# adaLN's first shift and scale: four of eight row sums as one-column products on PE

## The chip, the cores and the metric

One core of one Trainium2 chip runs the kernel. Its engines are PE (TensorE, matrix products), DVE (VectorE), ACT (ScalarE), POOL (GpSimd) and SP (SyncE, which here only issues transfers); each works through its own queue in order. The metric is device microseconds (us) of one execution; less is better.

## The reference, cut to what matters

The kernel computes one layer of a decoder trunk for 1024 tokens of 1024 channels in float32. Only its beginning matters here:

```python
cond = jax.nn.silu(c)
mod = cond @ w_ada[layer] + b_ada[layer]
shift1, scale1, gate1, shift2, scale2, gate2 = jnp.split(mod[:, None, :], 6, axis=-1)
h = rms_norm(x, w_norm1[layer]) * (1.0 + scale1) + shift1
proj = h @ w_in        # inside hybrid_mixer
```

`c` is one vector of 1024, `w_ada` is 1024 x 6144. `shift1` and `scale1` are sums over the 1024 rows of the first 2048 columns of `w_ada`. Every channel of `h` needs its shift and scale, and every later product needs `h`.

## The kernel before

Channels lie on 128 partitions in 8 blocks k, tokens in 8 tiles t. The first stage (lines 181 to 324) loads the x tiles, normalizes them in place (`x_rows`), transposes them on PE (`x_columns`) into `hT`, and then makes `h` in two parts whose sum has float32 accuracy: `hH` (rounded to the type fp32r in which PE multiplies) and `hL` (the rest). With them it computes `wva`, 272 columns of `w_in` (the attention's values and the gates), for all tokens, as `tok_hi` (`hH` by the weights' high and low parts) and `tok_lo` (`hL` by the high part), into eight PSUM tiles `os`.

The stage runs over four groups g of two channel blocks each (`GS`). For each group:
- SP loads the group's part of `w_ada` (`ada_load`) in two pieces `wt` of 512 rows, 2 x 512 KB each; `stw` has two buffers, so a load waits until the sums over an older piece are done.
- DVE multiplies each of 8 blocks of 128 rows by the column of `cond` and adds it up in `acc`, 128 partitions x 512 columns (`ada_sums`, lines 209 and 211): eight instructions.
- PE transposes `acc` in four pieces (line 289), and DVE reduces them over the partitions that were (line 290): this gives shift and scale with channels on partitions. Two small DVE instructions (292, 294) add `b_ada` and the gain to give `sc`.
- ACT makes `hH` = `hT` x scale + shift for two blocks, then `hT` the same way in place; POOL subtracts the two to give `hL` (line 304; in the last group DVE takes the second block).
- PE runs `tok_lo` of the group before, then `tok_hi` of this one.

The split of a raw weight tile `wraw` into `wh` (ACT) and `wl` (`split`, line 61) stands in the same queues. For `wva` itself POOL does the subtraction; for the weights of the next products DVE does. The order inside this stage is the order in which the code is written; work from behind it (loads and splits of the next weights, line 134 and 61) is placed among it by a scheduler. The PSUM pools are `ps` (2 banks) and `pq` (6).

Of the kernel before, what the change touches and what calls it, by code (L numbers as in the profile page):

```python
# [9 lines left out]
F32 = mybir.dt.float32  # L10
# [4 lines left out]
OP = mybir.AluOpType  # L15
# [21 lines left out]
def hybrid_block_kernel(ctx, tc, x, c, w_in, w_out, w_mix_norm, attn_f_bias, sg_w, sg_b,  # L37
# [143 lines left out]
    with tc.tile_pool(name="st", bufs=1, side="left") as st, tc.tile_pool(name="stx", bufs=6, side="left") as stx, \  # L181
            tc.tile_pool(name="stw", bufs=2, side="left") as stw, tc.manual_schedule():
        hT = st.tile([P, KT, S], F32, name="hT")
# [9 lines left out]
        def ada_load(g, q):  # L193

            k0, k1 = GS[g]
            was[g, q] = stw.tile([P, 4, 2, (k1 - k0) * P], F32, name=f"wt{k1 - k0}", tag="wt")
            for i in range(2):
                nc.sync.dma_start(was[g, q][:, :, i], w_ada[q * 4 * P:(q + 1) * 4 * P, i * D + k0 * P:i * D + k1 * P]
                                  .rearrange("(k p) f -> p k f", p=P))

        def ada_sums(g, q):
            if q == 0:
                n = GS[g][1] - GS[g][0]
                accs[g] = st.tile([P, 2, n * P], F32, name=f"acc{n}", tag="acc", bufs=2)
            acc = accs[g]
            for k in range(q * 4, q * 4 + 4):
                wt = was[g, q][:, k % 4]
                if k == 0:
                    nc.vector.tensor_scalar(acc, wt, cond[:, k:k + 1], None, op0=OP.mult)
                else:  # L210
                    nc.vector.scalar_tensor_tensor(acc, wt, cond[:, k:k + 1], acc, op0=OP.mult, op1=OP.add)

# [23 lines left out]
        for lo, hi, src in ((8, 16, w_norm1.rearrange("o (a p) -> (o a) p", p=P)),  # L236
# [4 lines left out]
            nc.sync.dma_start(rows[lo - 8:hi - 8], src)  # L241
        ada_load(0, 0)
        for t in range(4, 7):
            x_load(t)
        ada_load(0, 1)
        x_load(7)
        wraw = [stx.tile([P, 4, 272], F32, name="wraw1", tag="xt") for _ in range(2)]
        for i in range(2):
            o = 0
            for c0, n in ((AV, 260), (MDT, 4), (LI, 8)):  # L250
                nc.sync.dma_start(wraw[i][:, :, o:o + n], w_in[i * 512:(i + 1) * 512, c0:c0 + n]
                                  .rearrange("(k p) g -> p k g", p=P))
                o += n
        wva = [wp.tile([P, KT, 272], F32R, name=f"w{s}") for s in "hl"] + [272]
        crows = st.tile([8, P], F32, name="crows")
        nc.scalar.dma_start(crows, c.rearrange("o (a p) -> (o a) p", p=P))
# [7 lines left out]
        for t in range(NT + 1):  # L264
            if t < NT:
                x_rows(t)
            if t:
                x_columns(t - 1)
            if t in (5, 7):
                ada_sums(0, t // 7)  # L270
        psc = pq1()
# [4 lines left out]
        sc = st.tile([P, 2, KT], F32, name="sc")  # L276
        os = [ps1() for _ in range(PSB)] + [pq1() for _ in range(7 - PSB)]
        NGK = len(GS)
        for g, (k0, k1) in enumerate(GS):
            ks, n = slice(k0, k1), k1 - k0  # L280
            for q in range(2):
                if g:
                    ada_sums(g, q)
                if g + 1 < NGK:
                    ada_load(g + 1, q)
            acc = accs[g]
            o = pq1()
            for i in range(2 * n):
                nc.tensor.transpose(o[:, i * P:(i + 1) * P], acc[:, i // n, i % n * P:(i % n + 1) * P], ident)
            nc.vector.tensor_reduce(sc[:, :, ks], o[:, :2 * n * P].rearrange("p (i k f) -> p i k f", i=2, k=n),  # L290
                                    axis=AX.X, op=OP.add)
            nc.vector.tensor_add(sc[:, :, ks], sc[:, :, ks],
                                 cols[:, 54:70].rearrange("p (i k) -> p i k", i=2)[:, :, ks])
            nc.vector.scalar_tensor_tensor(sc[:, 1, ks], sc[:, 1, ks], 1.0, cols[:, 8 + k0:8 + k1],
                                           op0=OP.add, op1=OP.mult)

            for k in range(*GS[g - 1]) if g else ():
                for t in range(NT - 1):
                    tok_lo(os[t], wva, t, k)
            for k in range(k0, k1):  # L300
                act(hH[:, k, :], hT[:, k, :], AF.Identity, scale=sc[:, 1, k:k + 1], bias=sc[:, 0, k:k + 1])
            for k in range(k0, k1):
                act(hT[:, k, :], hT[:, k, :], AF.Identity, scale=sc[:, 1, k:k + 1], bias=sc[:, 0, k:k + 1])
                (nc.gpsimd if g + 1 < NGK or k % 2 == 0 else nc.vector).tensor_sub(hL[:, k, :], hT[:, k, :], hH[:, k, :].bitcast(F32))

            for k in range(k0, k1):
                for t in range(NT - 1):
                    tok_hi(os[t], wva, t, k)
        os.append(pq1())
        for k in range(KT):  # L310
# [1908 lines left out]
```

## Time and profile before

| | us |
|---|---|
| median of 3 runs | 1276.43 |
| the runs | 1275.05 to 1279.74 |
| the profiled execution, own time | 1279.96 |
| its span, first to last instruction | 1278.3 |
| PE busy in the span | 1159.6 (91%) |
| DVE busy | 806.7 (63%) |
| ACT busy | 589.4 (46%) |
| POOL busy | 345.8 (27%) |

The span is what the profiler saw between the first and the last instruction; the run's own time has some 1.7 us around it. Busy shares are means over the whole kernel, so a stage with another limit is read by itself: its waits, and the timeline of each engine. `PEclk` is the share of TensorE's full clock of 2.4 GHz that was granted; it has two levels, 0.50 (1.2 GHz) and 1.00, and a value between is a mean over both.

### The profile page before, as it was taken

The numbers are of one execution on the slowest core, as the hardware profiler recorded it, in microseconds if no ns is written. First come the engines' busy times: TensorE is split into PE (matmuls) and PEld (weight loads), VectorE is DVE, ScalarE is ACT, GpSimd is POOL, SyncE is SP. The second block draws the span as 40 slices with busy tenths as digits, with TensorE's granted clock in tenths as the row PEclk, the third lists the DMA queues.
The fourth block names the chain that finished last, engine by engine and source line by source line (L and its number), as shares of the span: only waits on it lengthen the run. The fifth ranks groups of instructions, "written<-read, shape, count | busy, mean of one in ns | idle before, by whom it ended". The sixth has DMA issues, their size and how long they took to land. (4 is left out here: it accounts for less than half of the span.)

```text
span 1278.3 us, 18648 instructions
## 1 busy us (share of the span) xinstructions
PE 1159.6 (91%) x6455; PEld 872.4 (68%) x6455; DVE 806.7 (63%) x1484; ACT 589.4 (46%) x909; POOL 345.8 (27%) x331
## 2 busy tenths in 40 slices
PE   4589889999999899999959999899999999999981
PEld 3577776889998788887747744468666666666561
DVE  6976766857743488488878941335445576665675
ACT  6442114354743488444437841224324555555453
POOL 2420000002201278333321953313222322222111
PEclk8889989999999999999969999999999999999996
DMA  9614874231221123575477999999879999999985
GB/s 266 210 34 153 260 261 118 75 95 50 67 68 34 42 59 106 197 280 198 152 298 288 335 334 368 373 391 367 314 241 352 376 383 392 387 390 378 356 309 223
DMA packets 97397, 306.04 MB, mean 239 GB/s; under 512 B 15923, under 2 KB 54573, under 8 KB 72717
## 3 DMA queue, kind: packets, MB, share of 16 engines
q1 hardware_dynamic: 85050, 284.47, 60.8%
q0 software_dynamic: 9120, 17.69, 5.8%
q10 hardware_dynamic: 3122, 2.56, 0.6%
q8 instruction: 57, 0.93, 0.3%
q14 instruction: 48, 0.39, 0.1%
HBM read 283.86 MB, written 32.62 MB: 248 GB/s over the span
## 5 line engine op out<-in xcount | busy, mean ns | idle before, releaser
L1647 POOL DMA_INDIRECT x_d<-yt,tabi x34 | 62.4, 1835 | 228.8 <-DVE yt L1621 174.7
L56 PE MATMUL ps<-wu,xTs 128*64 128x512 f32 x256 | 119.5, 599 | 3.0 <-DMA wu<-in_w_expert_up_dram 3.0
L56 PE MATMUL ps<-wg,xTs 128*64 128x512 f32 x256 | 120.0, 599 | 0.0
L56 PE MATMUL ps<-wh,hH 128*128 128x256 f32 (+1 forms) x336 | 97.8, 292 | 12.3 <-ACT hH L53 5.9
L56 PE MATMUL ps<-wl,hH 128*128 128x256 f32 (+1 forms) x336 | 96.6, 288 | 0.0
L56 PE MATMUL ps<-wh,hL 128*128 128x256 f32 (+1 forms) x336 | 96.2, 291 | 0.0
L56 PE MATMUL ps<-hH,wh 128*128 128x512 f32 x224 | 89.6, 400 | 0.4 <-ACT xbc L53 0.4
L56 PE MATMUL ps<-hL,wh 128*128 128x512 f32 x224 | 89.4, 399 | 0.0
L56 PE MATMUL ps<-hH,wl 128*128 128x512 f32 x224 | 89.1, 398 | 0.0
L56 PEld LDWEIGHTS ps<-wh,hH 128*128 128x128 f32 x336 | 65.7, 195 | 15.3 <-ACT hH L53 6.5
L56 PE MATMUL ps<-split,xTH 128*128 128x512 f32 x200 | 69.4, 403 | 1.2
L1638 POOL TENSOR_TENSOR yt<-yt,g2bc 128x1024 f32<-128x1024 f32 x14 | 33.7, 2409 | 130.6 <-ACT yt L53 114.5
L56 PEld LDWEIGHTS ps<-wg,xTs 128*64 128x64 f32 x256 | 32.0, 136 | 54.2 <-issue 50.5
L53 ACT ACT_TABLE_LOAD x47 | 60.3, 1283 | 17.6 <-DVE xbc L685 5.9
L56 PEld LDWEIGHTS ps<-wl,hH 128*128 128x128 f32 x336 | 65.2, 194 | 1.7 <-issue 1.6
L53 ACT ACTIVATE xTH<-pq 128x512 fp32r<-128x512 f32 x33 | 18.4, 593 | 102.2 <-PE pq L1662 102.2
L56 PEld LDWEIGHTS ps<-wh,hL 128*128 128x128 f32 x336 | 65.4, 197 | 0.0
L56 PE MATMUL ps<-wh,xTH 128*128 128x512 f32 (+1 forms) x156 | 64.2, 412 | 1.2 <-PEq L1867 0.5
L56 PE MATMUL ps<-wl,xTH 128*128 128x512 f32 (+1 forms) x156 | 61.5, 394 | 0.6 <-DVE wl L61 0.5
L53 ACT ACTIVATE sg<-ps 128x512 f32<-128x512 f32 (+1 forms) x32 | 18.9, 592 | 92.3 <-PE ps L56 50.6
L56 PE MATMUL pq<-wd,aTs 128*64 128x512 f32 x256 | 59.0, 597 | 2.6 <-PEq L1855 2.2
L56 PE MATMUL ps<-wh,xTL 128*128 128x512 f32 (+1 forms) x156 | 60.9, 391 | 0.0
(566 smaller groups left out, 3257.2 us busy)
## 6 DMA issues: line engine op xcount, KB each, us to landing
wg<-in_w_expert_gate_dram SPq DMA_DIRECT2D x64, 1024.0 KB
wu<-in_w_expert_up_dram SPq DMA_DIRECT2D x64, 1024.0 KB
wd<-in_w_expert_down_dram SPq DMA_DIRECT2D x64, 1024.0 KB
mw<-in_w_ada_dram SPq DMA_DIRECT2D x32, 512.0 KB
wraw<-in_w_in_dram SPq DMA_DIRECT2D x20, 512.0 KB
xt<-in_x_dram SPq DMA_DIRECT2D x16, 512.0 KB
wt<-in_w_ada_dram SPq DMA_DIRECT2D x16, 512.0 KB
woraw<-in_w_out_dram SPq DMA_DIRECT2D x16, 256.0 KB
```

Of the source, the lines that this page charges most:

```text
L53: return nc.scalar.activation(o, i, f, **kw)
L56: return nc.tensor.matmul(o, l, r, start=start, stop=stop)
L1638: nc.gpsimd.tensor_mul(yt[:, on_dve * 512:], yt[:, on_dve * 512:], g2bc[:, on_dve * 512:])
L1647: nc.gpsimd.indirect_dma_start(out=x1_d, out_offset=bass.IndirectOffsetOnAxis(ap=tok, axis=0), in_=yt, in_offset=None, bounds_check=S - 1, ...
```

## The change

Half of the rows of each group, blocks k = 4 to 7, are no longer summed on DVE. `ada_columns` multiplies them on PE: the 128x128 piece of `wt` is the stationary operand and one column of `cond` the moving one, so that the result comes out as a column of `ada` with channels on partitions. The blocks k = 0 to 3 are still summed on DVE into `acc`; a fifth product with a column of ones adds this sum over the partitions. The transposes and the reduction are gone. `ada` takes one `ps` bank until the last group; `os` has one tile in `ps` and six in `pq` instead, and its eighth tile takes the bank of `ada`.

Loads come in pieces of half the rows, 2 x 256 KB, with four buffers. The load of `wva`'s raw weights is issued by POOL instead of SP. `hT` is computed by DVE instead of ACT, and `hL` is shared: POOL takes the even block, DVE the odd one. The sums of the next group stand behind this on DVE, and its columns on PE stand between `tok_hi` of this group and `tok_lo`.

The diff, cut to its core:

```diff
-            tc.tile_pool(name="stw", bufs=2, side="left") as stw, tc.manual_schedule():
+            tc.tile_pool(name="stw", bufs=4, side="left") as stw, tc.manual_schedule():
...
-            was[g, q] = stw.tile([P, 4, 2, (k1 - k0) * P], F32, name=f"wt{k1 - k0}", tag="wt")
+            was[g, q] = stw.tile([P, 2, 2, (k1 - k0) * P], F32, name="wt")
             for i in range(2):
-                nc.sync.dma_start(was[g, q][:, :, i], w_ada[q * 4 * P:(q + 1) * 4 * P, i * D + k0 * P:i * D + k1 * P]
+                nc.sync.dma_start(was[g, q][:, :, i], w_ada[q * 2 * P:(q + 1) * 2 * P, i * D + k0 * P:i * D + k1 * P]
                                   .rearrange("(k p) f -> p k f", p=P))
 
-        def ada_sums(g, q):
-            if q == 0:
...
-            for k in range(q * 4, q * 4 + 4):
-                wt = was[g, q][:, k % 4]
+        def ada_sums(g):
+
+            accs[g] = st.tile([P, 2, (GS[g][1] - GS[g][0]) * P], F32, name="acc", bufs=2)
+            for k in range(4):
+                wt = was[g, k // 2][:, k % 2]
                 if k == 0:
...
+        def ada_columns(g):
+
+            k0, k1 = GS[g]
+            n = k1 - k0
+            for i in range(2):
+                for j in range(n):
+                    o, cs = ada[:, 4 * g + i * n + j:4 * g + i * n + j + 1], slice(j * P, (j + 1) * P)
+                    for k in range(4, KT):
+                        mm(o, was[g, k // 2][:, k % 2, i, cs], cond[:, k:k + 1], k == 4, False)
+                    mm(o, accs[g][:, i, cs], ones[:, 0:1], False, True)
...
         ada_load(0, 0)
+        ada_load(0, 1)
         for t in range(4, 7):
             x_load(t)
-        ada_load(0, 1)
+        ada_load(0, 2)
         x_load(7)
+        ada_load(0, 3)
...
-                nc.sync.dma_start(wraw[i][:, :, o:o + n], w_in[i * 512:(i + 1) * 512, c0:c0 + n]
+                nc.gpsimd.dma_start(wraw[i][:, :, o:o + n], w_in[i * 512:(i + 1) * 512, c0:c0 + n]
...
+        ada_load(1, 0)
+        ada_load(1, 1)
...
-            if t in (5, 7):
-                ada_sums(0, t // 7)
+            if t == 5:
+                ada_sums(0)
+            if t == 7:
+                ada_columns(0)
...
-            for q in range(2):
-                if g:
-                    ada_sums(g, q)
-                if g + 1 < NGK:
-                    ada_load(g + 1, q)
-            acc = accs[g]
-            o = pq1()
-            for i in range(2 * n):
-                nc.tensor.transpose(o[:, i * P:(i + 1) * P], acc[:, i // n, i % n * P:(i % n + 1) * P], ident)
-            nc.vector.tensor_reduce(sc[:, :, ks], o[:, :2 * n * P].rearrange("p (i k f) -> p i k f", i=2, k=n),
-                                    axis=AX.X, op=OP.add)
-            nc.vector.tensor_add(sc[:, :, ks], sc[:, :, ks],
+            if g + 1 < NGK:
+                ada_load(g + 1, 2)
+                ada_load(g + 1, 3)
+            if g + 2 < NGK:
+                ada_load(g + 2, 0)
+                ada_load(g + 2, 1)
+            nc.vector.tensor_add(sc[:, :, ks], ada[:, 4 * g:4 * g + 2 * n].rearrange("p (i k) -> p i k", i=2),
...
             for k in range(k0, k1):
-                act(hT[:, k, :], hT[:, k, :], AF.Identity, scale=sc[:, 1, k:k + 1], bias=sc[:, 0, k:k + 1])
-                (nc.gpsimd if g + 1 < NGK or k % 2 == 0 else nc.vector).tensor_sub(hL[:, k, :], hT[:, k, :], hH[:, k, :].bitcast(F32))
+                nc.vector.tensor_scalar(hT[:, k, :], hT[:, k, :], sc[:, 1, k:k + 1], sc[:, 0, k:k + 1],
+                                        op0=OP.mult, op1=OP.add)
+            for k in range(k0, k1):
+                (nc.vector if k % 2 else nc.gpsimd).tensor_sub(hL[:, k, :], hT[:, k, :], hH[:, k, :].bitcast(F32))
+            if g + 1 < NGK:
+                ada_sums(g + 1)
...
+            if g + 1 < NGK:
+                ada_columns(g + 1)
```

In the order rows below, a name is the tile that an instruction writes, the names behind the arrow are what it reads, and a number behind a name tells tiles apart. The first place is DVE's queue for the second group, from `sc` of the first group to `sc` of the second (`wl` is the split of the next weights). Before:

```order
L294 SCALAR_TENSOR_TENSOR sc<-sc,cols 128x2
L209 TENSOR_SCALAR acc_406<-wt_358,cond 128x512
L211 SCALAR_TENSOR_TENSOR acc_406<-wt_358,cond,acc_406 128x512 x3
L211 SCALAR_TENSOR_TENSOR acc_406<-wt_361,cond,acc_406 128x512 x4
L61 TENSOR_TENSOR wl<-wraw,wh 128x4x256
L290 TENSOR_REDUCE sc<-pq_421 128x2x2
```

On the same place of DVE's queue in the changed kernel:

```order
L305 SCALAR_TENSOR_TENSOR sc<-sc,cols 128x2
L314 TENSOR_SCALAR hT<-hT,sc 128x1024 x2
L317 TENSOR_TENSOR hL<-hT,hH 128x1024
L207 TENSOR_SCALAR acc<-wt,cond 128x512
L61 TENSOR_TENSOR wl<-wraw,wh 128x4x256
L209 SCALAR_TENSOR_TENSOR acc<-wt,cond,acc 128x512 x3
L303 TENSOR_TENSOR sc<-ps_201,cols 128x2x2
```

Four sums went; `hT` twice, one `hL` and the `wl` split now stand ahead of the remaining sums.

The second place is PE's queue at the border between the first and the second group (`ps_201` is `ada`, `ps_351` and `ps_380` are the first tile of `os`). Before:

```order
L56 MATMUL pq_357<-wh,hH 128x272
L56 MATMUL pq_357<-wl,hH 128x272
L289 MATMUL pq_421<-ident,acc_406 128x128 x4
L56 MATMUL ps_351<-wh,hL 128x272
L56 MATMUL ps_352<-wh,hL 128x272
```

PE at the same border in the changed kernel:

```order
L56 MATMUL pq_386<-wh,hH 128x272
L56 MATMUL pq_386<-wl,hH 128x272
L56 MATMUL ps_201<-cond,wt 128x1 x4
L56 MATMUL ps_201<-ones,acc 128x1
L56 MATMUL ps_201<-cond,wt 128x1 x4
L56 MATMUL ps_201<-ones,acc 128x1
L56 MATMUL ps_201<-cond,wt 128x1 x4
L56 MATMUL ps_201<-ones,acc 128x1
L56 MATMUL ps_201<-cond,wt 128x1 x4
L56 MATMUL ps_201<-ones,acc 128x1
L56 MATMUL ps_380<-wh,hL 128x272
```

Four transposes became twenty one-column products, of which the fifth is the first that reads `acc`.

The third place is PE's queue at the last x tiles, ahead of the first group (`pq_315` to `pq_337`, and `pq_328` to `pq_366`, take the last two tiles' transposes). Before:

```order
L225 MATMUL pq_315<-ident,xt 128x128 x4
L225 MATMUL pq_321<-ident,xt 128x128 x4
L225 MATMUL pq_331<-ident,xt 128x128 x4
L225 MATMUL pq_337<-ident,xt 128x128 x4
L272 MATMUL pq_343<-ident,rows 128x66
L289 MATMUL pq_364<-ident,acc_288 128x128 x4
```

PE at the last x tiles in the changed kernel:

```order
L234 MATMUL pq_334<-ident,xt 128x128 x4
L56 MATMUL ps_201<-cond,wt 128x1 x4
L56 MATMUL ps_201<-ones,acc 128x1
L56 MATMUL ps_201<-cond,wt 128x1 x4
L56 MATMUL ps_201<-ones,acc 128x1
L56 MATMUL ps_201<-cond,wt 128x1 x4
L56 MATMUL ps_201<-ones,acc 128x1
L56 MATMUL ps_201<-cond,wt 128x1 x4
L56 MATMUL ps_201<-ones,acc 128x1
L234 MATMUL pq_360<-ident,xt 128x128 x4
L234 MATMUL pq_366<-ident,xt 128x128 x4
L288 MATMUL pq_372<-ident,rows 128x66
```

The first group's products moved ahead of the last x tile's transposes; in the kernel before its transposes of `acc` stood behind them.

## Rows read from the trace of the kernel before

**Rows 1.** Stretch: length, PE, PEld, DVE, ACT, POOL busy us, PEclk, DMA, GB/s.

```profile
80.00:90.00 10.00, 10.00 (x58) 8.82 (x58) 7.75 (x31) 5.52 (x13) 0.00 (x0) 1.00 0.18 49
```

**Rows 2.** Waits of 0 to 180 us: engine, line, releaser, us, times, longest.

```profile
ACT hH L53 <- DVE sc L294: 26.0, 4, 8.0
...
DVE acc L211 <- DMA wt<-in_w_ada_dram: 1.0, 2, 0.5
```

**Rows 3.** ACT's timeline: start us, us, engine, line, operation, operands, count [idle before].

```profile
36.13 2.38 ACT L53 ACTIVATE hH<-hT,sc 128x1024 fp32r<-128x1024 f32 x2 [4.65 <-DVE sc L294]
...
60.80 2.38 ACT L53 ACTIVATE hH<-hT,sc 128x1024 fp32r<-128x1024 f32 x2 [6.99 <-DVE sc L294]
...
73.44 2.37 ACT L53 ACTIVATE hH<-hT,sc 128x1024 fp32r<-128x1024 f32 x2 [7.99 <-DVE sc L294]
```

**Rows 4.** PE's timeline, 42 to 85 us.

```profile
58.56 1.09 PE L289 MATMUL pq<-ident,acc 128*128 128x128 f32 x4 [5.40 <-DVE acc L211]
...
75.25 0.36 PE L56 MATMUL ps<-wh,hH 128*128 128x272 f32 x1
```

**Rows 5.** DVE's and POOL's timeline in the third group.

```profile
51.35 7.06 DVE L211 SCALAR_TENSOR_TENSOR acc<-wt,cond,acc 128x512 f32<-128x512 f32 x4 [0.52 <-DMA wt<-in_w_ada_dram]
...
51.67 5.40 POOL L304 TENSOR_TENSOR hL<-hT,hH 128x1024 fp32r<-128x1024 f32 x2 [6.30 <-ACT hT L53]
```

**Rows 6.** Groups of instructions (busy us, mean ns), then ns min/median/max of the sums.

```profile
L218 DVE TENSOR_SCALAR xt<-xt,rstd 128x1024 f32<-128x1024 f32 x8 | 6.0, 754 | 0.3
L304 POOL TENSOR_TENSOR hL<-hT,hH 128x1024 fp32r<-128x1024 f32 x7 | 18.8, 2698 | 22.5 <-ACT hT L53 22.5
L61 DVE TENSOR_TENSOR wl<-wraw,wh 128x1024 fp32r<-128x1024 f32 x9 | 11.0, 1221 | 7.5 <-ACT wh L53 7.5
...
L211 DVE SCALAR_TENSOR_TENSOR acc<-wt,cond,acc x28: 742/752/2769, 23.0 to 70.3; 128x512 f32<-128x512 f32 x28
L209 DVE TENSOR_SCALAR acc<-wt,cond x4: 474/482/486, 22.5 to 60.7; 128x512 f32<-128x512 f32 x4
```

**Rows 7.** A TENSOR_SCALAR beside POOL, far behind this stage; its min/median/max ns last.

```profile
581.36 1.28 POOL L1359 TENSOR_TENSOR h<-h,sh 128x512 f32<-128x512 f32 x1 [2.10 <-ACT h L53]
...
581.43 1.23 DVE L1203 TENSOR_SCALAR eoh<-eoh,rsc 128x8 f32<-128x8 f32 x1
...
L1203 DVE TENSOR_SCALAR eoh<-eoh,rsc x16: 222/232/1266, 549.7 to 650.0; 128x8 f32<-128x8 f32 x16
```

**Rows 8.** PE's weight loads of plain fp32 products of 32 columns, at two places.

```profile
552.58 0.30 PEld L56 LDWEIGHTS pq<-both,tri 128*128 128x128 f32 x2
552.80 0.30 PEld L56 LDWEIGHTS pq<-both,ones 128*128 128x128 f32 x2
...
649.27 0.50 PEld L56 LDWEIGHTS pq<-both,tri 128*128 128x128 f32 x2 [3.46 <-issue]
649.65 0.55 PEld L56 LDWEIGHTS pq<-both,ones 128*128 128x128 f32 x2
```

**Rows 9.** Stretches as in rows 1: two around rows 8, two of the stage.

```profile
552.50:553.20 0.70, 0.70 (x8) 0.62 (x7) 0.30 (x4) 0.48 (x4) 0.00 (x0) 1.00 0.91 386
649.20:650.20 1.00, 0.90 (x4) 0.92 (x4) 0.90 (x7) 0.00 (x0) 0.11 (x1) 0.50 1.06 397
...
27.60:31.00 3.40, 2.05 (x9) 1.78 (x9) 3.29 (x6) 2.11 (x3) 0.42 (x1) 0.50 0.94 284
58.40:61.80 3.40, 3.24 (x15) 3.27 (x16) 3.16 (x7) 1.00 (x1) 0.00 (x0) 0.51 0.66 201
```

**Rows 10.** Timeline ahead of the first group: PE, ACT, DVE, POOL.

```profile
26.31 1.07 PE L225 MATMUL pq<-ident,xt 128*128 128x128 f32 x8 [2.73 <-DVE xt L218]
...
29.39 2.10 ACT L53 ACTIVATE wh<-wraw 128x1088 fp32r<-128x1088 f32 x2
...
33.64 2.40 DVE L294 SCALAR_TENSOR_TENSOR sc<-sc,cols 128x2 f32<-128x2 f32 x1
...
30.57 5.45 POOL L61 TENSOR_TENSOR wl<-wraw,wh 128x1088 fp32r<-128x1088 f32 x2 [23.93 <-ACT wh L53]
```

More of the change, by code (lines that the diff above doesn't have):

```diff
@@ L195, in ada_load @@
             k0, k1 = GS[g]
-            was[g, q] = stw.tile([P, 4, 2, (k1 - k0) * P], F32, name=f"wt{k1 - k0}", tag="wt")
+            was[g, q] = stw.tile([P, 2, 2, (k1 - k0) * P], F32, name="wt")
             for i in range(2):
-                nc.sync.dma_start(was[g, q][:, :, i], w_ada[q * 4 * P:(q + 1) * 4 * P, i * D + k0 * P:i * D + k1 * P]
+                nc.sync.dma_start(was[g, q][:, :, i], w_ada[q * 2 * P:(q + 1) * 2 * P, i * D + k0 * P:i * D + k1 * P]
                                   .rearrange("(k p) f -> p k f", p=P))
-        def ada_sums(g, q):
-            if q == 0:
-                n = GS[g][1] - GS[g][0]
-                accs[g] = st.tile([P, 2, n * P], F32, name=f"acc{n}", tag="acc", bufs=2)
-            acc = accs[g]
-            for k in range(q * 4, q * 4 + 4):
-                wt = was[g, q][:, k % 4]
+        def ada_sums(g):
+            accs[g] = st.tile([P, 2, (GS[g][1] - GS[g][0]) * P], F32, name="acc", bufs=2)
+            for k in range(4):
+                wt = was[g, k // 2][:, k % 2]
                 if k == 0:
-                    nc.vector.tensor_scalar(acc, wt, cond[:, k:k + 1], None, op0=OP.mult)
+                    nc.vector.tensor_scalar(accs[g], wt, cond[:, k:k + 1], None, op0=OP.mult)
                 else:
-                    nc.vector.scalar_tensor_tensor(acc, wt, cond[:, k:k + 1], acc, op0=OP.mult, op1=OP.add)
+                    nc.vector.scalar_tensor_tensor(accs[g], wt, cond[:, k:k + 1], accs[g], op0=OP.mult, op1=OP.add)
+        def ada_columns(g):
[7 more added lines that the diff above has]
+                    mm(o, accs[g][:, i, cs], ones[:, 0:1], False, True)
         def x_rows(t):
@@ L250, in hybrid_block_kernel @@
             for c0, n in ((AV, 260), (MDT, 4), (LI, 8)):
-                nc.sync.dma_start(wraw[i][:, :, o:o + n], w_in[i * 512:(i + 1) * 512, c0:c0 + n]
+                nc.gpsimd.dma_start(wraw[i][:, :, o:o + n], w_in[i * 512:(i + 1) * 512, c0:c0 + n]
                                   .rearrange("(k p) g -> p k g", p=P))
                 o += n
+        ada_load(1, 0)
+        ada_load(1, 1)
         wva = [wp.tile([P, KT, 272], F32R, name=f"w{s}") for s in "hl"] + [272]
+        ada = ps1()
         crows = st.tile([8, P], F32, name="crows")
@@ L276, in hybrid_block_kernel @@
         sc = st.tile([P, 2, KT], F32, name="sc")
-        os = [ps1() for _ in range(PSB)] + [pq1() for _ in range(7 - PSB)]
+        os = [ps1()] + [pq1() for _ in range(6)]
         NGK = len(GS)
@@ L280, in hybrid_block_kernel @@
             ks, n = slice(k0, k1), k1 - k0
-            for q in range(2):
-                if g:
-                    ada_sums(g, q)
-                if g + 1 < NGK:
-                    ada_load(g + 1, q)
-            acc = accs[g]
-            o = pq1()
-            for i in range(2 * n):
-                nc.tensor.transpose(o[:, i * P:(i + 1) * P], acc[:, i // n, i % n * P:(i % n + 1) * P], ident)
-            nc.vector.tensor_reduce(sc[:, :, ks], o[:, :2 * n * P].rearrange("p (i k f) -> p i k f", i=2, k=n),
-                                    axis=AX.X, op=OP.add)
-            nc.vector.tensor_add(sc[:, :, ks], sc[:, :, ks],
+            if g + 1 < NGK:
[5 more added lines that the diff above has]
+            nc.vector.tensor_add(sc[:, :, ks], ada[:, 4 * g:4 * g + 2 * n].rearrange("p (i k) -> p i k", i=2),
                                  cols[:, 54:70].rearrange("p (i k) -> p i k", i=2)[:, :, ks])
@@ L308, in hybrid_block_kernel @@
                     tok_hi(os[t], wva, t, k)
-        os.append(pq1())
+            if g + 1 < NGK:
+                ada_columns(g + 1)
+        os.append(ps1())
         for k in range(KT):
```

## The prediction

> **What bounds the kernel now.** I read the stretches of ten microseconds first, then the waits of the first 180 us, then the timeline of each engine for 20 to 84 us. From 80 us on PE is busy in all of every 10 us [rows 1], so the kernel's end moves one for one with the moment at which PE reaches that steady work; what lies before is the only place where this change can act. In the stage before, the longest wait is that of ScalarE's `hH` for `sc`: 26.0 us in four pieces [rows 2]. So the stage is a chain of four groups: DVE sums, a little PE and DVE work that makes `sc`, ACT's `hH`, PE's products. The four `hH` start at 36.13, then on to 60.80 and 73.44 [rows 3]: one group costs (73.44 - 36.13) / 3 = 12.4 us. PE sits idle for 5.40 us ahead of the transposes of `acc` [rows 4], and DVE waited for the loads of `wt` for only 1.0 us in all [rows 2]: the bound is DVE, not DMA and not PE.
>
> Why DVE needs 12 us for eight sums of 0.75 us [rows 6]: four of them took 7.06 us, while POOL ran its two subtractions for `hL` in 5.40 us [rows 5]. The longest single sum took 2.77 us, the shortest 0.74 [rows 6]: DVE stands until POOL's instruction of 2.70 us [rows 6] has ended. Another pair shows it for a TENSOR_SCALAR: it started 0.07 us after a POOL subtraction of 1.28 us, took 1.23 us where its median is 0.23, and ended with it [rows 7].
>
> **The change, part by part.** Let A be the start of a group's `hH`.
>
> *Sums halved.* Four of eight sums per group leave DVE: 4 x 0.75 = 3.0 us, and the reduction of the transposes with them. DVE also takes up work: two `hT` (128x1024 TENSOR_SCALAR, 0.75 us each as the same shape in line 218 [rows 6]) and one `hL` subtraction (no free row of this shape on DVE in this stage; the split `wl` of 128x1024 is the same operation, 1.22 us [rows 6]). That is 2.7 us: DVE's work hardly falls, and ACT and POOL are relieved, which nobody waits for.
>
> *Order on DVE.* The order rows show that all of this stands ahead of the next group's sums, and the `wl` split too, which before came behind them. The chain: `hH` of the first k is done at A+1.24 (2.38 for two [rows 3]); `hT` until A+2.05; POOL starts its one subtraction at A+2.1 and holds it for 2.70, until A+4.8. The second `hT` could start at A+2.4 but stands behind POOL and ends about 0.55 after it, at 5.35; subtraction 1.22, first sum 0.48, `wl` 1.22, three sums 2.26 [rows 6]: the sums end at A+10.5. The waits of DVE on ACT are covered by nothing, as ACT's `hT` fell away and `hH` is first in its queue. The held TENSOR_SCALAR has rows only for 8 elements [rows 7]. If one of 1024 were not held, the subtraction behind it, which has two inputs like the held sums, still would be: 0.65 us less, 2 us over three groups. By the Trainium skill, GPSIMD Engine Reference, its table of the engine (SBUF interfaces), DVE contends with POOL in a 2-port mode or with two SBUF inputs; by it both are held and the sum stands as it is.
>
> *Columns on PE.* A group has 4 columns of 4 + 1 plain fp32 products, 20 in all; each runs as two passes with a 128x128 weight load. No row has one moving column; the nearest are products of 32 columns: two of them start 0.22 us apart at a granted clock of 1.00, and 0.38 us apart at 0.50 [rows 8, 9]. A weight load of 128 columns fills nearly all of that, so I take 0.22 and 0.38; 0.12 a product would be the lower bound if the load were half hidden. By the Trainium skill, TensorE: Matmul & The Clock Gate, LDWEIGHTS, a load costs its columns over 1.2 GHz, 107 ns for 128, with no word of the clock: 0.21 a product. The rows agree at 1.00 and differ at 0.50; by the page the half clock would cost the columns nothing, and the sum below would be some 4 us lower.
>
> Of the 20, four run ahead; the fifth needs `acc` and PE, in order, stands until the sums end. So 16 x 0.22 = 3.5 us lie on the path, behind DVE, where before four transposes and a reduction lay. With 0.15 for the hand-over and 0.6 from PE's last to `hH` (59.65 to 60.80 before, 1.15, less the reduction that goes [rows 3, 4]), the new group is 10.5 + 0.15 + 3.5 + 0.6 = 14.75 us against 12.4. Queued behind the waiting product on PE are the 14 `hL` products of the group; they fit between the last column and the next `hH` and cost nothing at full clock.
>
> *The first group.* `ada_columns(0)` stands on PE ahead of the transposes of the last x tile. It can begin when the transposes of the tile before end, 26.31 + 1.07 = 27.4 [rows 10]. The clock granted at 27.6 to 31.0 was 0.50 [rows 9]: 9 products in those 3.6 us, then 11 at 0.22: they end at t = 33.4 (31.8 at full clock, 35.2 at half). Then the last x tile's first transposes (half of 1.07), ACT's copy of them (512 elements, by half a split of 1088 some 0.55), two splits of 1.05 [rows 10] and 0.2 of hand-over: A0 = t+3.4 at the earliest, 36.8, against 36.13. POOL's two `wl` splits, 5.45 us [rows 10], now run from t+2.3 to t+7.75 and so beside group 0 itself. Before, they ended as `hH` began: a tiny DVE sum for `sc` stood 2.40 us behind them [rows 10]. Now whatever DVE does for group 0 waits: `hL` on POOL until t+10.45, DVE's subtraction until t+11.5, 0.48 + 1.22 + 2.26 more: the sums of group 1 end at t+15.5, and A1 = t+19.75 = 53.15. With two periods of 14.75, A3 = 82.65, against 73.44: +9.2 us.
>
> *The clock.* PE is idle from about A+5.7 to A+10.5, nearly 5 us. After the idle 5.40 us of before, the next 3.4 us were granted 0.51 [rows 4, 9]. A stretch of 3.4 us at half costs 1.7 us of products; for three groups I charge half of it, 2.5 us.
>
> *Loads.* Pieces of half the size leave the bytes as they are. The last two pieces of a group wait for PE's last column of the group before (about A-0.6): 1.05 MB at 284 GB/s [rows 9] is 3.7 us, and DVE holds the column that follows until A+10.5, a cover of over 5 us. The `w_in` load of 1.1 MB goes from SP's queue to POOL's, past SP's last x tile and two pieces of `wt`: from 1.8 us earlier (0.5 MB less ahead of that x tile) to 2.1 us later (all 1.1 MB ahead). I take 0 and keep the ends. By the Trainium skill, DMA: Bandwidth & Descriptors, Issuing engines are not separate DMA queues, another queue brings no bandwidth; no run here shows it.
>
> *After the stage.* PE went on at 75.25, 1.8 us after the last `hH` [rows 3, 4]; now 1.3 to 2.6. Zero taken. The sum: 9.2 + 2.5 = +12 us (11.7). The profiled run took 1279.96 us around a span of 1278.3, so 1292; the median of the runs shown is 1276.43, 3.5 lower, so 1288.
>
> **The rivals.**
>
> *R1, the clock stays low.* The columns and what follows run at 0.50 throughout: t = 35.2 (+1.8), 16 x 0.16 = 2.6 more in each of three groups, 0.8 at the end, in place of the 2.5: 9.2 + 10.4 = +20, 1296. For it: at 27.6 to 31.0 and at 649 us, amid short pieces of work, the clock was at 0.50 [rows 9], and no row shows what a one-column product does to it. Against it: the products of 32 columns at 552 us ran at 1.00 [rows 9].
>
> *R2, POOL does not hold DVE; not slower.* If shapes of 1024 elements pass beside POOL, the second `hT` ends at A+3.15 and the sums at A+8.4; the group is 8.4 + 4.25 = 12.65, A0 = 36.8, A3 = 74.8: +1.3, 1278. It decides where DVE's chain falls by 2.3 us a group. Against it: rows 5 and 7.
>
> *R3, faster.* R2, and a product costs 0.12: t = 29.8, A0 = 33.2, group 8.4 + 0.75 + 1.9 = 11.05, A3 = 66.4: -7, 1269. Each half alone does not get there: 0.12 with DVE held gives 13.1 a group.
>
> *R4, the change does not do what it says:* the last pieces arrive late and PE's columns wait for DMA instead of DVE. It needs over 5 us of delay a group; inside it, nothing is seen, beyond it each us counts whole: all three late by 2 us beyond it is +6 on top of the forecast, +18, 1294.
>
> **How the numbers follow.** Forecast (+5 to +16): 0.52. R1: 0.18. R4: 0.03. R2 with what lies up to +6: 0.20. R3: 0.07. A measurement of this kernel can tell about 0.5% (6.4 us) from no change. Slower by more: the forecast, R1 and R4, 0.73; within: R2, 0.20; faster: 0.07. The range leaves out R3 and the ends of R1 and of the late load (+22): 1277 to 1298.
>
> **What would show it.** In the profile after: the four `hH` some 14 to 17 us apart, where 12.4 stood; DVE's second `hT` of each group at about 3 us instead of 0.75, ending with POOL's subtraction; PE idle ahead of its first `acc` column, about 5 us, put down to DVE; 20 columns in 4.4 us at 1.00; the first `hH` at 36 to 40 us. Wrong would be: `hH` 12.6 us or less apart, a free second `hT`, or PE waiting for `wt`; then the forecast's term for DVE or for PE falls.

## The result, and the profile after

The changed kernel takes 1294.56 us (median of 4 runs, 1290.37 to 1299.15) against 1278.09 us for the kernel before, measured beside it: a ratio of 1.0128, 95% interval 1.0106 to 1.0151. It is 16.5 us slower. Its profiled execution took 1296.38 us around a span of 1294.7.

The four `hH` of ACT's timeline answer to [rows 3] (start us, us, engine, line, operation, operands, count, idle before and its releaser):

```profile
41.78 2.37 ACT L53 ACTIVATE hH<-hT,sc 128x1024 fp32r<-128x1024 f32 x2 [1.68 <-DVE sc L305]
...
59.95 2.38 ACT L53 ACTIVATE hH<-hT,sc 128x1024 fp32r<-128x1024 f32 x2 [14.85 <-DVE sc L305]
...
76.33 2.38 ACT L53 ACTIVATE hH<-hT,sc 128x1024 fp32r<-128x1024 f32 x2 [13.06 <-DVE sc L305]
...
90.25 2.38 ACT L53 ACTIVATE hH<-hT,sc 128x1024 fp32r<-128x1024 f32 x2 [11.54 <-DVE sc L305]
```

They stand 18.2, 16.4 and 13.9 us apart, where 12.4 was the mean before. The first is 5.65 us late, the last 16.8, and the profiled time grew by 16.4: all of the loss is made in this stage, about a third of it ahead of the first `hH`. From 100 us on PE is busy without a gap at full clock, as it was from 80 us on in [rows 1].

The waits of 0 to 180 us answer to [rows 2]:

```profile
ACT hH L53 <- DVE sc L305: 41.1, 4, 14.8
...
DVE sc L303 <- PE ps L56: 12.9, 2, 7.1
```

ACT's wait for `sc` grew from 26.0 to 41.1 us, and behind it now stands a wait of DVE for PE's columns. The same view of 24 to 100 us has no line in which DVE or PE waits for a `wt`, so no late piece of `w_ada` is in it.

One full group on DVE and POOL, from `hH` at 59.95 on, and the PE rows that follow, answer to [rows 4, 5]. In the PE rows a product is counted twice, once for each pass, so x8 is four products:

```profile
61.23 0.81 DVE L314 TENSOR_SCALAR hT<-hT,sc 128x1024 f32<-128x1024 f32 x1 [1.31 <-ACT hH L53]
62.36 2.68 DVE L314 TENSOR_SCALAR hT<-hT,sc 128x1024 f32<-128x1024 f32 x1 [0.32 <-ACT hH L53]
65.08 1.23 DVE L317 TENSOR_TENSOR hL<-hT,hH 128x1024 fp32r<-128x1024 f32 x1
66.22 0.48 DVE L207 TENSOR_SCALAR acc<-wt,cond 128x512 f32<-128x512 f32 x1
66.61 1.22 DVE L61 TENSOR_TENSOR wl<-wraw,wh 128x1024 fp32r<-128x1024 f32 x1
67.75 2.32 DVE L209 SCALAR_TENSOR_TENSOR acc<-wt,cond,acc 128x512 f32<-128x512 f32 x3
...
62.12 2.37 POOL L317 TENSOR_TENSOR hL<-hT,hH 128x1024 fp32r<-128x1024 f32 x1 [14.50 <-DVE hT L314]
```

```profile
70.13 0.38 PE L56 MATMUL ps<-ones,acc 128*128 128x1 f32 x2 [2.10 <-DVE acc L209]
70.37 1.03 PE L56 MATMUL ps<-cond,wt 128*128 128x1 f32 x8
71.27 0.36 PE L56 MATMUL ps<-ones,acc 128*128 128x1 f32 x2
71.49 1.85 PE L56 MATMUL ps<-cond,wt 128*128 128x1 f32 x8
```

The second `hT` takes 2.68 us and ends 0.55 us behind POOL's subtraction (62.12 + 2.37 = 64.49, against 65.04). The sums end at 70.07, 10.1 us after `hH` began. PE then starts the column's fifth product at once. Four products take 0.90 us at first (70.37 to 71.27), and 1.71 us a moment later (71.49 to 73.20): 0.225 against 0.427 us each.

The windows show why (length, busy us of PE, PEld, DVE, ACT, POOL, granted clock, DMA share, GB/s); they answer to [rows 9]:

```profile
28.00:36.00 8.00, 8.00 (x40) 8.00 (x39) 1.52 (x3) 1.12 (x4) 0.00 (x0) 0.50 0.57 181
...
52.50:59.50 7.00, 6.97 (x33) 6.97 (x33) 0.00 (x0) 0.00 (x0) 0.00 (x0) 0.50 0.56 191
...
72.00:76.00 4.00, 4.00 (x20) 4.00 (x20) 0.06 (x1) 0.00 (x0) 0.00 (x0) 0.50 0.53 179
85.40:88.00 2.60, 2.51 (x23) 2.51 (x23) 0.04 (x1) 0.00 (x0) 0.00 (x0) 1.00 0.00 0
88.00:94.00 6.00, 6.00 (x30) 6.00 (x31) 3.36 (x12) 2.38 (x2) 2.15 (x3) 0.55 0.01 3
```

These stretches are the one-column products and what follows them. In the first three PE is busy all of the time and yet has 0.50 of its clock, that is 1.2 GHz. At 85.4 a set of them began at 1.00 and ran without a gap; by 88 to 94 the mean was 0.55.

The first group, in rows of PE, DVE, POOL and ACT, answers to [rows 10]:

```profile
27.99 1.71 PE L56 MATMUL ps<-cond,wt 128*128 128x1 f32 x8
...
36.38 1.95 PE L234 MATMUL pq<-ident,xt 128*128 128x128 f32 x8
...
39.42 2.26 DVE L305 SCALAR_TENSOR_TENSOR sc<-sc,cols 128x2 f32<-128x2 f32 x1
...
39.19 4.94 POOL L61 TENSOR_TENSOR wl<-wraw,wh 128x1088 fp32r<-128x1088 f32 x2 [20.50 <-ACT wh L53]
...
27.28 1.06 ACT L53 ACTIVATE sq<-xt 128x1024 bf16<-128x1024 f32 x1 [3.57 <-DMA xt<-in_x_dram]
```

The 20 products of group 0 fill 27.99 to 36.38, 8.4 us, and the last x tile's transposes come behind them. The tiny product for `sc` is held by POOL's split for 2.26 us; ACT, which has its own splits to do until 40.1, stands 1.68 us of this ahead of `hH`. And ACT waited 3.57 us for the last x tile; in the kernel before that tile's squares began 3.06 us earlier:

```profile
24.22 1.06 ACT L53 ACTIVATE sq<-xt 128x1024 bf16<-128x1024 f32 x1 [0.86 <-DMA xt<-in_x_dram]
```

### The profile page after: what moved, and what is told of

The parts are those of the page before. It is cut to its first block, busy times and chain, and to the rows that moved or that the text cites. A ratio compares the mean times of both kernels' runs of the same rounds, so it can differ in the third digit from the quotient of the medians.

```text
span 1294.7 us, 18933 instructions
## 1 busy us (share of the span) xinstructions
PE 1188.1 (92%) x6599; PEld 902.1 (70%) x6599; DVE 795.8 (61%) x1475; ACT 580.1 (45%) x901; POOL 339.2 (26%) x334
## 5 line engine op out<-in xcount | busy, mean ns | idle before, releaser
L61 DVE TENSOR_TENSOR wl<-wu,wh 128x1024 fp32r<-128x1024 f32 x39 | 47.1, 1223 | 20.3 <-ACT wh L53 19.6
```

The source lines that it names most:

```text
L61: (eng or nc.vector).tensor_sub(lo, src, hi.bitcast(F32))
```

## The experiments

Theory at the start: the order on DVE together with POOL's hold puts the sums late, PE waits for them, and 16 products lie behind. The rivals were the clock alone, and the loads. Each run was profiled once; the table gives for each profile the first `hH`, the three distances, the last `hH`, the time, and the time less the last `hH`.

| kernel | first | distances | last | time | rest |
|---|---|---|---|---|---|
| before | 36.13 | 11.96, 12.71, 12.64 | 73.44 | 1279.96 | 1206.5 |
| changed | 41.78 | 18.17, 16.38, 13.92 | 90.25 | 1296.38 | 1206.1 |
| e1_sums_first | 40.57 | 13.70, 12.12, 12.79 | 79.18 | 1280.45 | 1201.3 |
| e2_wide | 38.06 | 19.40, 15.05, 13.63 | 86.14 | 1288.08 | 1201.9 |
| e6_loads_alone | 41.02 | 11.98, 12.43, 12.45 | 77.88 | 1285.38 | 1207.5 |
| e7_late_columns | 40.60 | 16.52, 16.00, 16.27 | 89.39 | 1287.82 | 1198.4 |
| e3_no_pool | 42.71 | 16.84, 15.91, 12.93 | 88.39 | 1290.47 | 1202.1 |
| e10_load_back | 39.34 | 13.80, 12.44, 11.95 | 77.53 | 1284.27 | 1206.7 |
| e11_load_back_wide | 36.48 | 11.50, 9.97, 10.30 | 68.25 | 1273.03 | 1204.8 |
| e12_load_back_wide_hT_act | 36.11 | 11.50, 9.96, 10.16 | 67.73 | 1272.16 | 1204.4 |
| t4_six_sums | 36.29 | 9.72, 9.50, 9.69 | 65.20 | 1272.14 | 1206.9 |

The rest is the same work in all of them and still varies from 1198 to 1208 us (t1 to t3, which repeat kernels of the table, had 1205 to 1208), and 30 runs of the kernel before lie between 1269.35 and 1286.03. One single time can't tell differences below some 8 us, so single runs are judged by the stage's own times, and four kernels were timed ten times each. The first `hH` of one and the same code also varies from run to run: 36.11 and 37.71 for the kernel of e12, where ACT had the fifth x tile at 17.14 and at 19.13; and 40.57 to 42.71 in the changed kernel, e1, t1 and e3, whose code is the same up to there.

### The order on DVE

```
+            if g + 1 < NGK:            # right behind the product that makes sc
+                ada_sums(g + 1)
             for k in range(*GS[g - 1]) if g else ():
...
-            if g + 1 < NGK:            # behind hT and hL
-                ada_sums(g + 1)
```

> The changed kernel with the four sums of group g+1 on DVE moved from behind the hL subtractions to right behind the scale of group g; nothing else. Theory A (the order on DVE plus GpSimd's hold put the sums late, and PE waits for them before the column of the sums): the PE idle time of 2.9, 2.1 and 0.7 us ahead of the product with acc goes, the sums end some 4 us after the scale and the hH of the four groups stand about 16, 14 and 13 us apart instead of 18.2, 16.4 and 13.9; the last hH comes 5 to 6 us earlier, at about 84.5. Theory B (the 20 one-column products themselves at the clock of 0.50, 8.5 us a group, are the bound, and DVE only fills their time): the same 5.7 us at most, and the 20 products stay at 0.43 us each. Theory C (the weight pieces come too late for earlier sums): a wait of DVE for wt of over 1 us appears and the last hH stays at 90.

Measured: distances of 13.70, 12.12 and 12.79, the last `hH` at 79.18, 11.1 us earlier than in the changed kernel, twice the gain expected. Of this 9.9 us is in the distances; 1.2 lies ahead of the first `hH`, where the edit changes nothing. The same window of the two kernels, the changed one first, tells why:

```profile
44.00:76.00 32.00, 27.04 (x149) 26.87 (x149) 17.18 (x19) 4.43 (x5) 5.37 (x3) 0.66 0.42 133
```

```profile
44.00:76.00 32.00, 32.00 (x206) 32.00 (x204) 19.65 (x25) 5.70 (x5) 13.12 (x3) 0.73 0.52 164
```

PE's 5 us of idle time are gone, as the theory had it, and the granted clock went from 0.66 to 0.73 as well. The two go together: removing the wait won more than the wait. PE is now the bound, busy in all of the 32 us. The 20 products of the three groups took 5.6, 4.9 and 4.4 us, not the 8.5 of theory B, and DVE waits for no piece of `wt`, so theory C falls too. Theory A named the right wait, but its gain left out the clock. The kernel was timed again:

> The kernel of e1_sums_first again, timed in rounds. Its last hH stood 11.1 us earlier than the changed kernel's and 5.7 us later than that of the kernel before. Theory A (what comes behind the stage follows one to one): 1282 to 1285, 0.3 to 0.6% over the kernel before. Theory B (the single time of 1280.45 was right, since the clock behind the stage is higher than in the changed kernel): 1279 to 1281, no difference that can be measured.

Measured: 1282.20 us (10 runs, 1275.65 to 1286.18) against 1279.38 for the kernel before (30 runs, 1269.35 to 1286.03), ratio 1.0016, interval 0.9987 to 1.0044. The median lies at the lower edge of theory A; it cannot be told from the kernel before. This one move takes back nearly all that the change lost.

### POOL's hold

```
-                (nc.vector if k % 2 else nc.gpsimd).tensor_sub(hL[:, k, :], ...)
+                nc.vector.tensor_sub(hL[:, k, :], ...)
```

> The changed kernel with both hL subtractions of each group on DVE, none on GpSimd. Theory A (the second hT and what follows it on DVE stand until GpSimd's subtraction of 2.4 us has ended): the second hT takes 0.8 us instead of 2.68, the second subtraction adds 1.22, and the sums end at A + 9.4 instead of A + 10.1, A being the start of a group's hH. Theory B (the second hT is slow for a reason of its own, as its wait for hH or the width of its rows): it stays near 2.7 us and the sums end 1.2 us later, at A + 11.3.

```profile
60.82 0.81 DVE L314 TENSOR_SCALAR hT<-hT,sc 128x1024 f32<-128x1024 f32 x1 [1.31 <-ACT hH L53]
61.96 0.81 DVE L314 TENSOR_SCALAR hT<-hT,sc 128x1024 f32<-128x1024 f32 x1 [0.32 <-ACT hH L53]
62.69 2.35 DVE L317 TENSOR_TENSOR hL<-hT,hH 128x1024 fp32r<-128x1024 f32 x2
...
66.49 2.33 DVE L209 SCALAR_TENSOR_TENSOR acc<-wt,cond,acc 128x512 f32<-128x512 f32 x3
```

With POOL out of the groups the second `hT` takes 0.81 us instead of 2.68, and the sums end at 68.82, 9.27 us after `hH` at 59.55 (expected 9.4). Theory A holds: the hold is real, also for a TENSOR_SCALAR of 1024 elements, and it is worth less than 1 us a group here, because DVE does POOL's work instead.

### The clock

```
-    mm(o, was[g, k // 2][:, k % 2, i, cs], cond[:, k:k + 1], k == 4, False)
-    mm(o, accs[g][:, i, cs], ones[:, 0:1], False, True)
+    mm(o, was[g, k // 2][:, k % 2, i, cs], cond[:, k:k + 1].to_broadcast([P, P]), k == 4, False)
+    mm(o, accs[g][:, i, cs], ones, False, True)      # o: 128 columns, one of them is read
```

> The changed kernel with every one-column product replaced by the same product with 128 equal columns (cond spread over 128 columns, ones for the sum), of which one is read; weight loads, order and waits are the same. Theory A (PE at work on one-column products, though busy all the time, does not raise the granted clock; 128 columns do): the granted clock in the stretch from 30 to 38 us rises from 0.50 to near 1.00 and the products go at 0.25 us or less there, so that the first hH comes 3 us or more earlier than 41.78. Theory B (the clock does not depend on the columns; it is what PE did before): the clock stays at 0.50 from 28 to 36, products take 0.43 us or more each, the first hH at 42 or later and the last at 90 or later.

The windows of the run, then two of its PE rows:

```profile
28.00:32.00 4.00, 4.00 (x20) 4.00 (x20) 1.52 (x3) 1.42 (x4) 0.00 (x0) 0.50 1.05 332
32.00:36.00 4.00, 4.00 (x35) 3.83 (x33) 0.00 (x0) 0.44 (x1) 0.00 (x0) 0.94 0.13 34
80.00:96.00 16.00, 14.16 (x113) 13.95 (x114) 8.54 (x25) 5.60 (x11) 3.03 (x3) 1.00 0.00 2
```

```profile
30.77 1.86 PE L56 MATMUL ps<-cond,wt 128*128 128x128 f32 x8
...
33.81 1.06 PE L56 MATMUL ps<-cond,wt 128*128 128x128 f32 x8
```

In 32 to 36 us the clock is at 0.94, where the changed kernel stayed at 0.50 from 28 to 36 us; from 80 to 96 us it is 1.00 throughout, where the changed kernel had 0.73:

```profile
80.00:96.00 16.00, 15.26 (x95) 15.17 (x95) 10.62 (x19) 2.38 (x2) 3.79 (x4) 0.73 0.00 1
```

Theory A holds for the clock. The first `hH` came 3.7 us earlier, the last 4.1. Not all of the 3.7 is the products' speed, though: the product for `sc` now ended just before POOL's first split began, so that ACT had no wait for it, where it stood 1.68 us in the changed kernel:

```profile
37.05 0.16 DVE L305 SCALAR_TENSOR_TENSOR sc<-sc,cols 128x2 f32<-128x2 f32 x1
...
37.24 5.40 POOL L61 TENSOR_TENSOR wl<-wraw,wh 128x1088 fp32r<-128x1088 f32 x2 [18.90 <-ACT wh L53]
```

At equal clock 128 columns cost no more than one: four products take 0.90 us at 1.00 in both forms (33.81 to 34.71 here, 70.37 to 71.27 above). In the first distance, 19.4 us, the gain is not kept: POOL's splits of `wl`, which began only at 37.24, hold DVE's chain for group 1, and the idle time of PE ahead of `acc` grew to 4.72 us, with 0.50 again behind it. This suggests that the clock and DVE's order have to be mended together, which the runs under "All causes together" test.

### The loads

The kernel before, with the smaller pieces, the four buffers and POOL's queue of the change. One thing of the change's loads it does not have: all four pieces of group 0 stay ahead of the last x tile, where the change puts the last of them behind it.

```
-    tc.tile_pool(name="stw", bufs=2, ...)      # pieces of 512 rows
+    tc.tile_pool(name="stw", bufs=4, ...)      # pieces of 256 rows
...
-    nc.sync.dma_start(wraw[i][:, :, o:o + n], ...)
+    nc.gpsimd.dma_start(wraw[i][:, :, o:o + n], ...)
```

> The kernel before with only the loads of the change: pieces of 256 rows of w_ada in four buffers, and the 272-column raw weights from GpSimd's queue instead of SyncE's. All eight sums stay on DVE and the transposes on PE. Theory A (loads cost next to nothing in the groups): the first hH within 1 us of 36.13, the last within 2 us of 73.44, the whole time within 3 us of the kernel before. Theory B (the later landing of the last block of x, 3.0 us in the changed kernel, is passed on one to one): hH 3 us late throughout, 1281 instead of 1278.

```profile
28.96 1.06 ACT L53 ACTIVATE sq<-xt 128x1024 bf16<-128x1024 f32 x1 [4.45 <-DMA xt<-in_x_dram]
...
41.02 2.37 ACT L53 ACTIVATE hH<-hT,sc 128x1024 fp32r<-128x1024 f32 x2 [4.88 <-DVE sc L295]
```

The last x tile's squares begin 4.74 us later than before, the first `hH` comes 4.89 us later, and the distances stay as they were. Theory B, and more than it said: the loads are not free; alone they cost what the last x tile is late. Some of these 4.9 us can come from the piece that still stands ahead of it; with the change's own order the x tile was 2.5 to 4.4 us late (changed kernel, e1, e2, e3, e7, t1). In the changed kernel that x tile is scaled by 29.6 us, but PE's columns run until 36.38, so there the lateness is hidden behind the columns. Next, the columns out of the way of that x tile, on the changed kernel:

```
-            if t == 7:
+            if t == NT:
                 ada_columns(0)
```

> The changed kernel with the 20 products of group 0 moved behind the transposes of the last block of x on PE; nothing else. Theory A (the first hH is 5.65 us late because these products, 8.4 us at the clock of 0.50, stand ahead of the last transposes and of what DVE and ACT make of them): the transposes of the last block end about 8 us earlier, the products overlap the evictions and splits behind, and the first hH comes at 38 to 40 instead of 41.78, with the rest moved by as much. Theory B (the products end last wherever they stand, being 8.4 us from the landing of the last piece): the first hH stays within 1 us of 41.78.

Measured: first `hH` at 40.60, just outside both theories. It is no gain either: e1 and t1, with the products in their old place, had 40.57 and 40.64. The transposes moved ahead, to 29.37, but could not start earlier, since the x tile was late; the 20 products then took 31.11 to 39.5, again at 0.50:

```profile
31.11 1.70 PE L56 MATMUL ps<-cond,wt 128*128 128x1 f32 x8
...
39.07 0.56 PE L56 MATMUL ps<-ones,acc 128*128 128x1 f32 x2
```

So two causes cover each other: with the late x tile alone (e6) or the products ahead of it taken away (e7), the first `hH` stays at 40.6 us or later. With the sums first, the columns behind, and the raw weights back on SP's queue (the two edits above, and):

```
-    nc.gpsimd.dma_start(wraw[i][:, :, o:o + n], ...)
+    nc.sync.dma_start(wraw[i][:, :, o:o + n], ...)
```

> The changed kernel with three edits: sums of group g+1 right behind the scale of group g, the products of group 0 behind the transposes of the last block of x, and the 272-column raw weights back on SyncE's queue. Theory A (the raw weights on GpSimd's queue go ahead of the last block of x and are what made it land 3.0 us late; the kernel before with all of the new loads was 5.0 us late at the first hH): the last block's squares start near 24.2 instead of 27.28 and the first hH comes at 36 to 38.5. With the spacing of the kernel with the sums first alone, 13.7, 12.1 and 12.8, the last hH stands at 75 to 77 and the time at 1277 to 1281. Theory B (the smaller pieces, not the queue, make x late): the first hH stays at 40 or later and the last at 79 or later.

```profile
23.35 1.05 ACT L53 ACTIVATE sq<-xt 128x1024 bf16<-128x1024 f32 x1
```

The last x tile is there without a wait, with the smaller pieces still in place: it was POOL's queue, as theory A says. In the changed kernel POOL and SP issued the raw weights and that x tile at the same time, and the x tile came last:

```profile
14.21 4.48 POOL L262 DMA_DIRECT2D wraw<-in_w_in_dram  x6 [7.62 <-DVE xt L227]
...
15.01 0.80 SPq L191 DMA_DIRECT2D xt<-in_x_dram  x1
```

The Trainium skill, DMA: Bandwidth & Descriptors, Issuing engines are not separate DMA queues, says that transfers started by different engines run on the same 16 DMA engines and interleave; the landing 2.5 to 4.7 us later in the runs with POOL's queue agrees. The first `hH` came at 39.34, later than the 38.5 expected, as the 20 products at 0.50 took 8.4 us behind the transposes; the last `hH`, 77.53, and the time, 1284.27, came out above theory A as well. Timed ten times:

> The kernel of e10_load_back again, timed in rounds. Its last hH stood 1.7 us earlier than that of e1_sums_first, but its single time was 3.8 us longer. Theory A (the time follows the last hH, single times differ by some us for reasons behind the stage): 1 to 2 us below t1_sums_first, 1280 to 1284. Theory B (something behind the stage costs this kernel 4 us): some 4 us above t1_sums_first.

Measured: 1282.56 us (10 runs, 1273.55 to 1286.75), ratio 1.0023, interval 0.9991 to 1.0056: not to be told from the kernel before nor from t1_sums_first. Theory B's 4 us do not show, as the medians differ by 0.36 us; but the ten runs of each spread over 10 to 13 us, so a gain or a loss of some 3 us in this combination is neither shown nor excluded.

### All causes together

As e10_load_back, with the 128 columns of e2_wide:

```
-    ... cond[:, k:k + 1], k == 4, False)
+    ... cond[:, k:k + 1].to_broadcast([P, P]), k == 4, False)
```

> As the run e10_load_back, and every one-column product as one of 128 equal columns. Theory A (with the sums first PE is the bound, busy in all of 44 to 84 us, and its 40 passes a group run at the clock of 0.50 for half of their time): with the clock at 1.00 a group is 28 x 0.127 of hH products, 20 x 0.225 of columns and 14 x 0.125 of hL products, 9.8 us; the hH stand 10 to 11 us apart, the last at 67 to 70, and the time is 1270 to 1275. Theory B (the clock gains nothing, since PE is not the bound or the wide products do not raise it): the spacing stays at 12 to 13.7 and the time within 3 us of e10_load_back.

```profile
44.00:76.00 32.00, 31.70 (x261) 31.11 (x261) 22.23 (x34) 9.39 (x8) 9.75 (x6) 1.00 0.39 127
```

261 PE instructions in the window where the changed kernel did 149, at 1.00 instead of 0.66. The last two distances, 9.97 and 10.30, are close to what PE's work in a group adds up to, 9.8 us; the first, 11.50, is longer than theory A's 11. The last `hH` at 68.25 and 1273.03 us are both as theory A had them. With `hT` on ACT again:

```
-    nc.vector.tensor_scalar(hT[:, k, :], hT[:, k, :], sc[:, 1, k:k + 1], sc[:, 0, k:k + 1], ...)
+    act(hT[:, k, :], hT[:, k, :], AF.Identity, scale=sc[:, 1, k:k + 1], bias=sc[:, 0, k:k + 1])
```

> As the run e11_load_back_wide, with hT back on ACT, as in the kernel before. Theory A (DVE is no longer the bound once the sums stand first): within 1 us a group of e11_load_back_wide, last hH and time alike. Theory B (DVE's chain is still what PE waits for): each group 1.5 us shorter, the last hH 4 us or more earlier.

Distances within 0.15 us of e11_load_back_wide: theory A, DVE is no longer the bound. The same kernel timed ten times:

> The kernel of e12_load_back_wide_hT_act again, timed in rounds. Its last hH stood 5.7 us earlier than that of the kernel before. Theory A: 1271 to 1274, 0.4 to 0.7% below the kernel before. Theory B (single times mislead): within 0.3% of the kernel before.

Measured: 1274.62 us (10 runs, 1270.75 to 1277.02), ratio 0.9963, interval 0.9936 to 0.9990: at the edge of theory A, half of what the single times had shown. Last, six blocks of rows on DVE and two on PE:

```
-            for k in range(4):                     # ada_sums
+            for k in range(6):
...
-                    for k in range(4, KT):         # ada_columns
+                    for k in range(6, KT):
```

> The kernel of t3_wide_hT_act with six of the eight row blocks summed on DVE and two on PE: 12 products a group instead of 20. Theory A (with the sums first and the clock at 1.00, PE's 10 us a group are the bound): 8 x 0.225 = 1.8 us less a group on PE, DVE has 1.5 more and stays below it; the hH stand 8.2 to 8.8 us apart instead of 10.0, the first comes 1.5 to 3 us earlier, since its products run at half clock at first, and the last at 60 to 63; the time is 1265 to 1268. Theory B (the pieces of w_ada then come too late, or DVE's chain with 1.5 us more takes PE's place): spacing of 9.5 or more, the last hH at 65 or later, 1269 to 1273.

```profile
46.41 6.12 DVE L210 SCALAR_TENSOR_TENSOR acc<-wt,cond,acc 128x512 f32<-128x512 f32 x5
...
49.59 2.39 POOL L321 TENSOR_TENSOR hL<-hT,hH 128x1024 fp32r<-128x1024 f32 x1 [6.83 <-DVE acc L210]
...
52.58 0.49 PE L56 MATMUL ps<-ones,acc 128*128 128x128 f32 x2 [1.07 <-DVE acc L210]
```

Measured: 1270.36 us (10 runs, 1265.05 to 1274.57), ratio 0.9930, interval 0.9902 to 0.9958: the lowest median of all, below both kernels; against t3_wide_hT_act, 4.3 us higher, the spreads still overlap. The distances are theory B's, 9.5 to 9.7, and so is the time. The pieces of `w_ada` are not late, so it is the other half of theory B. Its five sums behind the first take 6.12 us where 3.9 would be free: they now reach into POOL's subtraction, DVE stands for 2.2 us, and PE waits 1.07 us for `acc`. DVE took PE's place as the bound, by the hold again. The first `hH`, 36.29, did not come earlier, as theory A had it would: POOL's split held the product for `sc` there, 1.65 us.

## Why the prediction was right in part

The direction was right, the chain on DVE was the one forecast, and the time lay inside the range. The time forecast, 1288, was 6.6 us short, and R1's 1296 was nearer; of the 6.6, 1.7 is that the kernel before had a median of 1276.43 then and 1278.09 beside the result. Of the signs named, the held second `hT` came; distances of 18.2 and 13.9 lie outside 14 to 17, PE's idle time was smaller, most columns did not run at 1.00, and the first `hH` was late. The range held because it had room for R1's clock, not because the sum was right.

**Right: DVE's chain.** The sums were to end at A + 10.5; they ended at A + 10.1, and at A + 9.1 in the third group, which has no `wl`. The second `hT` ended 0.55 us behind POOL, as worked out. Moving the sums ahead (e1_sums_first) brought 11.1 us of the 16.8 back, 9.9 of it in the distances; without POOL (e3_no_pool) the hold was gone. R2 is out. One step of the working is 0.2 us short: `hL` on POOL until t+10.45 and a subtraction of 1.22 end at t+11.67, not t+11.5.

**Right: a product's cost follows the clock, 0.22 us at 1.00 and 0.38 at 0.50.** It measured 0.225 and 0.427; the 0.38 came from one pair of loads behind an idle time [rows 8] and was 0.05 us too low. The Trainium skill, TensorE: Matmul & The Clock Gate, LDWEIGHTS, gives the load a cost without a word of the clock; by it the half clock would have cost the products nothing, and here it cost nearly twice. The bound of 0.12 fell, and R3 with it.

**Mis-sized: the clock.** It was charged 2.5 us, from the one stretch behind an idle time that the rows of before held [rows 4, 9]. Against the forecast the columns of group 0 took 2.4 us more (8.4 instead of 6.0), and from the end of the sums to the next `hH` it took 7.48, 6.26 and 4.81 us instead of 4.25, 5.8 us more in all: 8.2 us. The forecast had counted on the clock of 1.00 for products that got 0.50 while PE was busy. The last `hH` was put at 85.15 with the charge (82.65 + 2.5) and stood at 90.25, 5.1 us later: 8.2 less the 2.5 charged, 0.6 for a later start of group 0's columns, 0.6 for the first sums, less 1.8 by which DVE was faster in the later groups. R1 was the better reading of the clock, but not true throughout: 1.00 was granted at 64 to 68 us in part, and at 85.4 to 88.

**Missed: the first group.** The first `hH` was to come at 36 to 40 us and came at 41.78. "36.8 at the earliest" had left out that POOL's split, put by the prediction itself at t + 2.3 on, would hold the product for `sc`, 2.26 us, as it had before [rows 10]; ACT stood 1.68 us for it. With t at 36.38 instead of 33.4, this makes most of the 5.0 us. It is not in the sum for the last `hH`, which went by POOL's splits.

**Wrong, and hidden: the loads at 0.** The last x tile was late by 2.5 to 4.7 us in the runs with POOL's queue, beyond the upper end of 2.1. In the changed kernel the columns covered it, so it did not show in the time, which is luck; alone it is 4.9 us (e6_loads_alone, whose last x tile stands behind one more piece). The cover over the pieces of `wt` held: R4 is out.

**PE's idle time** ahead of `acc` was 2.86, 2.10 and 0.74 us instead of 5: the products before it filled it. The `hL` products of the group before ran at 0.50 and ended at 62.70, 2.75 us after the second `hH` began, and the `hH` products ran at 0.50 in part. The wait was smaller because the work was slower.

**Not settled:** why one-column products come with 0.50. Shown is that in the same place and order products of 128 columns came with 0.94 from 32 us on and with 1.00 from 80 us on (e2_wide). One column does not always mean 0.50: in e1_sums_first the last set of 20 ran at 1.00 from 73.78 to 78.16, behind `hH` products that were at 1.00 from 71.6 us on.

## What to carry to other kernels

Work that is moved from a full engine to an idle one must not come to lie behind that full engine in the same chain: half the sums left DVE, but the other half stood behind `hT` and `hL`, and where they stood was worth 9.9 us over three groups (e1_sums_first). Read the granted clock of the place the work is moved to, and ask what it will be under this work and not after some busy time. Where two causes cover each other, undo both before calling either harmless.

## What was not expected of the hardware

- One moving column or 128: a plain fp32 product with a new 128x128 weight load takes 0.225 us at a granted clock of 1.00 and 0.427 at 0.50 in both. But PE busy from 28 to 36 us with one column stayed at 0.50, and at the same place with 128 columns it had 0.50 in the first half and 0.94 in the second.
- The hold between DVE and POOL goes both ways. In e1_sums_first POOL's subtraction, which takes 2.37 us in the changed kernel, began beside DVE's `hT` and took 5.12:

```profile
46.37 5.12 POOL L319 TENSOR_TENSOR hL<-hT,hH 128x1024 fp32r<-128x1024 f32 x1 [3.45 <-DVE hT L316]
...
45.48 1.53 DVE L316 TENSOR_SCALAR hT<-hT,sc 128x1024 f32<-128x1024 f32 x2
46.92 1.22 DVE L61 TENSOR_TENSOR wl<-wraw,wh 128x1024 fp32r<-128x1024 f32 x1
48.06 1.22 DVE L319 TENSOR_TENSOR hL<-hT,hH 128x1024 fp32r<-128x1024 f32 x1
```

There DVE's instructions went at their free time (0.77 us for each `hT`, 1.22 for the split and for the subtraction), and POOL stood: it ended at 51.49, 2.2 us after the last of them.
